# Two sibling edits joined: the end of the convolution module, the dilated closing, and a fifth place for weight units

## The chip, the cores and the metric

The kernel runs on one core of one Trainium2 chip. The metric is the device time of one execution in microseconds; several executions are taken and their median is compared. A profile of one execution stands beside them.

## The reference

Two transformer blocks of two layers each run over 512 tokens of 1024 features, all in float32. What matters here, shortened:

```python
for l in range(2):                                    # first block
    x = x + rmsnorm(mixer(rmsnorm(x)) @ w_out, norm_mix_post[l])
    x = x + rmsnorm(conv_gated_mlp(rmsnorm(x)), norm_ffn_post[l])
# second block, layer 0: conformer module
u = h @ w_in + b_in
u = u[..., :1024] * sigmoid(u[..., 1024:])
u = causal_dwconv(u, dw, dw_b)                        # 31 taps for each channel
u = silu(layer_norm(u, ln_g, ln_b))
x = x + rms_norm(u @ w_out + b_out, mix_post_g)
x = x + rms_norm(conv_ffn(rms_norm(x)), ffn_post_g)
# layer 1: dilated attention of 8 heads, then @ w_o, then the same feed-forward
```

## The kernel before, in words

Every product is done in three matmuls of a high and a low part (fp32r): x high by w high, x high by w low (or the reverse), x low by w high. Weights come from one packed tensor `in_wall` in the order of `PLAN`, eight 128 x 128 tiles to a unit. `dma_to` (L265 on) loads a unit on SyncE's queue into one of three `raw` tiles; `split_to` makes its two parts, a copy on ScalarE (L301) and a subtraction on VectorE (L302), ahead of the unit's use. Ordinary units go into four `w` tiles. Units marked keep go into tiles that `keeper` gives, since they are used while the four `w` tiles hold other units: the last four units of each closing, and the first four after it. `hold` says up to which unit kept ones may be split yet; `behind` names, for ScalarE and VectorE, an instruction behind which the steps of kept units are queued (`queue_behind`).

The program is a sequence of stages: mixer, feed-forward (`ffn`), mixer, feed-forward, `conformer`, feed-forward, `dilated`, feed-forward. Each ends in `closing`: a product with 1024 outputs, done for the first 256 tokens (h = 0), then for the other 256 (h = 1), each followed by `norms`: residual sum, post-norm, and `pre_norm`, which squares x, takes the inverse square root in some twelve small VectorE steps (`inv_sqrt`), makes xn (L473 on VectorE, L477 on ScalarE), transposes it on PE (htp, L488) and splits it into hh (L728) and hl (L729). `head` then runs the first six output tiles of the next stage over both halves. The last feed-forward has no next stage; its last two token tiles end in `last_norm` (L443 on), which adds, squares, multiplies by the gain in place (L451), and writes out.

In `conformer` eight channel tiles pass `conv_inputs`. Tiles 0 to 2 are summed tap by tap on VectorE (`tap_sums`, L1325), tiles 3 to 7 by matmuls with banded matrices on PE (`conv`, L1349), whose input cup is a rearranged copy of cu made by 16 small transfers (L1301). Each finished tile vc is transposed (ctp), copied to vt by token (L1369, L1334) and enters the statistics (L1373, L1336). Then come the aggregates (L1378), the inverse square root, and the normalisation of vt, q = 0 and 2 on VectorE (L1393), q = 1 and 3 on ScalarE (L1389). `silu_tiles` transposes back (ltp, L1236), applies silu (L1241) and splits into ch and cl, and the closing's matmuls (L555 to L557) use them.

In `dilated` the heads run first, then `close_begin` does the first four of the closing's eight steps while the last head's softmax runs, and `closing` the rest.

What order the instructions take on an engine is fixed when the program is built, by a planner that works with estimated times and keeps dependencies; on the chip each engine takes its instructions in that order. The generators of norms and convolutions are called in turns by a clock of spent PE time (`spend`, `tick`), which sets the order in which the code offers its work to the planner.

Of the kernel before, what the change touches and what calls it, by code (L numbers as in the profile page):

```python
# [28 lines left out]
P = 128  # L29
# [13 lines left out]

CONV_M, CONV_PAD = 9, 8

CONV_DVE, CONV_TAP = 3, 1.0
AX_LANES, AX_SOFTMAX, AX_NEXT, AX_PROB = 2, 5.5, 2.0, 1.7
AX_PM = 4
WIN_LANES, WIN_NEXT, WIN_SOFTMAX, WIN_PROB = 2, 2.0, 3.9, 1.4
# [175 lines left out]
class Kernel:  # L225
# [217 lines left out]
    def last_norm(self, t, banks, y, gain):  # L443

        nc = self.nc
        sums = self.sm.tile([P, 2, 2], F32, tag="sums", name="sums", bufs=4)[:, :1]
        halves = [(y[:, t, n * S : (n + 1) * S], slice(n * S, (n + 1) * S)) for n in range(2)]
        for n, (to, _) in enumerate(halves):
            nc.vector.tensor_tensor(to, to, banks[n], op=OP.add)
            self.square(to, sums[:, 0, n : n + 1])  # L450
        nc.vector.tensor_tensor(y[:, t], y[:, t], gain, op=OP.mult)  # L451
        rs = self.rms(sums)
        for n, (to, cols) in enumerate(halves):
            nc.vector.scalar_tensor_tensor(
                self.x[:, t, cols], to, rs[:, 0:1], self.x[:, t, cols], op0=OP.mult, op1=OP.add
            )
            queue = nc.scalar if n else nc.sync
            queue.dma_start(self.out[t * P : (t + 1) * P, cols], self.x[:, t, cols])

    def pre_norm(self, h, gain, wait=(0.0, 0.0)):  # L460
# [9 lines left out]
        for i in range(2):  # L470
            xn.append(self.sp.tile([P, D], F32, tag="xn", name="xn", bufs=2))
            if i:
                last = nc.vector.tensor_scalar(  # L473
                    xn[i], self.x[:, 2 * h + i], rs[:, i : i + 1], None, op0=OP.mult
                )
            else:
                last = nc.scalar.activation(  # L477
                    xn[i], self.x[:, 2 * h + i], AF.Copy, scale=rs[:, i : i + 1]
                )
            if h == 0 and self.n_unit:  # L480
                self.behind[last.ins.engine] = last.ins
        yield NORM_SUM[h] + NORM_NEXT
        at = slice(h * HS, (h + 1) * HS)
# [126 lines left out]
            self.close_some(xs, units, banks, 0, [k], [(0, 0), (0, 1), (1, 0)], 0, KD - 1)  # L610
        return banks, units

    def closing(self, w, l, xs, y, gain, pre, bias=None, ready=None, begun=None):


        groups, last = out_groups(len(xs))
# [3 lines left out]
        with self.tc.tile_pool(name="tail", bufs=1, reuse_waits="tile") as tp:  # L620
# [6 lines left out]
            else:  # L627
                banks, units = begun
            done = len(units)
            self.hold = self.n_unit + KD - done  # L630
            for k in range(done, KD):
                units += self.take_units(gemm_tiles(w, l, range(8), [last[k]]))
                if ready is not None:
# [25 lines left out]
    def ffn(self, up, down, l, taps, shifts, cb, act, post, pre):  # L659
        nc, tc = self.nc, self.tc  # L660
        groups, last = out_groups(NFF)
        with (
            tc.tile_pool(name="ffn", bufs=1, reuse_waits="tile") as fp,
            tc.tile_pool(name="taps", bufs=1, reuse_waits="tile") as qp,
        ):
            y = fp.tile([P, 4, D], F32, tag="y", name="y")
            gain = self.row(fp, post)

# [42 lines left out]
            for i, ks in enumerate(groups):  # L711
                got = group(ks)
                self.close_group(down, l, ks, got, y, i == 0)
                acts += got
            acts += group(last)
            with tc.tile_pool(name="kept", bufs=1, side="right", reuse_waits="tile") as tp:
                self.keeper(tp, "wt", 4)
                self.closing(down, l, acts, y, gain, pre)


    def split_out(self, hi, lo, src, scale=None):
# [434 lines left out]
    def mixer(self, l):  # L1156
        nc, tc = self.nc, self.tc
        with tc.tile_pool(name="mix", bufs=1, reuse_waits="tile") as yp:
# [35 lines left out]
            with tc.tile_pool(name="merged", bufs=1, reuse_waits="tile") as gp:  # L1194
                mh = gp.tile([P, KD, S], F32R, tag="mh", name="mh")
                ml = gp.tile([P, KD, S], F32R, tag="ml", name="ml")
                gain = self.row(gp, f"norm_mix_post{l}")
                self.branch(l, 2, yc, macc, False, (mh, ml))
                self.keeper(yp, "ys", 4)
                y = yp.tile([P, 4, D], F32, tag="macc", name="y")  # L1200
                self.closing(
                    "w_out", l, [(mh[:, k], ml[:, k]) for k in range(KD)], y,
                    gain, f"norm_ffn_pre{l}",
                )


# [46 lines left out]
    def conv_inputs(self):  # L1253
# [54 lines left out]
        def tap_sums():  # L1308
            for j in range(CONV_DVE):
# [26 lines left out]
                    nc.vector.bn_stats(stats[:, q, j], by[:, q])  # L1336
                summed.append(j)

        def conv():
            for j in range(CONV_DVE, KD):  # L1340
                while min(j + 1, KD - 1) not in phased:
                    yield 0.5
                if j == KD - 1:
                    yield 2.0
                ps = self.psum("a", "conv")
                for i in range(4):
                    w = mats[j][:, i]
                    for m in range(CONV_M):
                        nc.tensor.matmul(  # L1349
                            ps[:, i * P : (i + 1) * P], w[:, m].rearrange("p a b -> p (a b)"),  # L1350
                            phased[j][:, i, CONV_PAD - m : CONV_PAD - m + P],
                            start=m == 0, stop=m == CONV_M - 1, skip_group_check=True,
                        )
                    self.spend(CONV_M * 0.218)
                    yield 0.0
                if j + 2 < KD:
                    matrices(j + 2)
                vc = cv.tile([P, 4, P], F32, tag="vc", name="vc", bufs=3)
                nc.vector.tensor_tensor(
                    vc, ps.rearrange("p (i s) -> p i s", i=4),  # L1360
                    bias[:, 4 * j : 4 * j + 4, None].to_broadcast([P, 4, P]), op=OP.add,
                )
                yield 1.5
                pt = self.psum("a", "ctp")
                for i in range(4):
                    nc.tensor.transpose(pt[:, i * P : (i + 1) * P], vc[:, i], self.ident)
                self.spend(0.45)
                by = pt.rearrange("s (i q c) -> s q i c", i=4, q=4)
                nc.scalar.activation(  # L1369
                    vt[:, :, j * P : (j + 1) * P].rearrange("s q (i c) -> s q i c", i=4), by, AF.Copy  # L1370
                )
                for q in range(4):
                    nc.vector.bn_stats(stats[:, q, j], by[:, q])  # L1373
            while len(summed) < CONV_DVE:
                yield 0.3
            mv = self.sm.tile([P, 4, 2], F32, tag="lmv", name="lmv")
            for q in range(4):
                nc.vector.bn_aggr(mv[:, q], stats[:, q].rearrange("p a b -> p (a b)"))  # L1378
# [5 lines left out]
            nc.vector.scalar_tensor_tensor(  # L1384
                sh, mv[:, :, 0], -1.0, rs, op0=OP.mult, op1=OP.mult
            )
            for q in range(4):
                if q % 2:
                    nc.scalar.activation(  # L1389
                        vt[:, q], vt[:, q], AF.Identity, scale=rs[:, q : q + 1], bias=sh[:, q : q + 1]  # L1390
                    )
                else:
                    nc.vector.tensor_scalar(  # L1393
                        vt[:, q], vt[:, q], mv[:, q, 0:1], rs[:, q : q + 1],
                        op0=OP.subtract, op1=OP.mult,
                    )

        matrices(CONV_DVE)
        matrices(CONV_DVE + 1)
# [149 lines left out]
    def dilated(self):  # L1549
        with self.tc.tile_pool(name="dily", bufs=1, reuse_waits="tile") as yp:  # L1550
# [1 line left out]
            yl = yp.tile([P, KD, S], F32R, tag="dyl", name="dyl")  # L1552
            xs = [(yh[:, k], yl[:, k]) for k in range(KD)]
            gain = self.row(yp, "mix_post_g1")
            begun = self.dilated_heads(xs)
            with self.tc.tile_pool(name="kept", bufs=1, side="right", reuse_waits="tile") as tp:
                self.keeper(tp, "wt", 4)
                y = tp.tile([P, 4, D], F32, tag="y", name="y")
                self.closing("w_o", 0, xs, y, gain, "ffn_pre_g1", begun=begun)

    def dilated_heads(self, xs):
        nc, tc = self.nc, self.tc
# [222 lines left out]
```

## Time and profile before

| | us |
| --- | --- |
| median of 3 executions | 3178.2 (3178.11 to 3181.9) |
| the profiled execution | 3177.36 |
| its span, first to last instruction | 3175.6 |
| PE busy | 3103.4 |
| VectorE busy | 1828.9 |
| ScalarE busy | 1360.2 |

Busy times are unions of an engine's instructions. Matmuls follow each other before the earlier ones end, so a busy PE is one that has work under way. Times in the rows are microseconds from the span's start; line numbers are those of the kernel before.

### The profile page before, as it was taken

To read this page: it belongs to the slowest core of one execution; us is meant where nothing else is said; L and a number is where in the kernel's file an instruction comes from. 1 tells how busy PE (TensorE), PEld (TensorE's weight loads), DVE (VectorE), ACT (ScalarE), POOL (GpSimd) and SP (SyncE) were. 2 spreads that over 40 slices of the span, in tenths; PEclk is the share of its full clock that TensorE was granted. 3 is DMA by queue.
4 is the path that set the end of the run, shared out by engine and by line. 5 is a ranking of instruction groups with operands and counts; after the bars stand their busy time and mean duration, and the time that the engine had idled before them with its cause. 6 is when DMAs were issued, how large, how long until landed. Compare 5 with 4: busy or idle time off the path is not lost. (4 is left out here: it accounts for less than half of the span.)

```text
span 3175.6 us, 40474 instructions
## 1 busy us (share of the span) xinstructions
PE 3103.4 (98%) x15764; PEld 2609.7 (82%) x15764; DVE 1828.9 (58%) x3337; ACT 1360.2 (43%) x2231; POOL 337.1 (11%) x350
## 2 busy tenths in 40 slices
PE   8999999999999999999999989999999999999998
PEld 7788888888878888888888878888888888888887
DVE  6778346455676754555556865456545545464555
ACT  5566244334456643444334244334533333353332
POOL 0211100000011111000000000000143333100000
PEclk9999999999999999999999999999999999999999
DMA  4222232333311223233324422333222222223332
GB/s 139 67 77 84 94 106 85 95 100 94 99 64 60 90 90 107 79 100 98 95 93 161 152 87 73 97 95 120 74 87 73 75 86 80 74 87 99 95 99 73
DMA packets 86543, 293.84 MB, mean 93 GB/s; under 512 B 11088, under 2 KB 13904, under 8 KB 86352
## 3 DMA queue, kind: packets, MB, share of 16 engines
q1 hardware_dynamic: 82896, 278.41, 27.4%
q10 hardware_dynamic: 3456, 12.85, 1.1%
q8 instruction: 124, 2.03, 0.3%
q14 instruction: 67, 0.55, 0.0%
HBM read 287.81 MB, written 2.10 MB: 91 GB/s over the span
## 5 line engine op out<-in xcount | busy, mean ns | idle before, releaser
L345 PE MATMUL mm<-hh,w 128*128 128x512 f32 (+1 forms) x2720 | 1051.3, 386 | 0.0
L347 PE MATMUL mm<-hh,w 128*128 128x512 f32 (+1 forms) x2720 | 1035.7, 381 | 0.0
L346 PE MATMUL mm<-hl,w 128*128 128x512 f32 (+1 forms) x2720 | 1035.0, 381 | 0.0
L302 DVE TENSOR_TENSOR w<-raw,w 128x1024 fp32r<-128x1024 f32 x436 | 570.4, 1309 | 431.0 <-ACT w L301 426.4
L347 PEld LDWEIGHTS mm<-hh,w 128*128 128x128 f32 x2720 | 511.6, 188 | 97.0 <-issue 1.9
L346 PEld LDWEIGHTS mm<-hl,w 128*128 128x128 f32 x2720 | 512.4, 188 | 89.7 <-issue 1.9
L345 PEld LDWEIGHTS mm<-hh,w 128*128 128x128 f32 x2720 | 512.1, 188 | 89.8 <-issue 1.9
L301 ACT ACTIVATE w<-raw 128x1024 fp32r<-128x1024 f32 x436 | 458.5, 1053 | 236.8 <-PE mm L557 172.1
L679 DVE SCALAR_TENSOR_TENSOR cg<-mm,vecs,cg 128x511 f32<-128x511 f32 (+1 forms) x176 | 131.9, 749 | 207.0 <-ACT cg L672 204.3
L557 PE MATMUL mm<-w,al 128*128 128x512 f32 x576 | 224.7, 390 | 0.0
L555 PE MATMUL mm<-w,ah 128*128 128x512 f32 x576 | 224.6, 390 | 0.0
L556 PE MATMUL mm<-w,ah 128*128 128x512 f32 x576 | 224.6, 390 | 0.0
L679 DVE SCALAR_TENSOR_TENSOR cv<-mm,vecs,cv 128x511 f32<-128x511 f32 (+1 forms) x176 | 131.9, 749 | 103.9 <-ACT cv L672 101.2
L282 POOL TENSOR_TENSOR raw<-raw,vecs 128x1024 f32<-128x1024 f32 x66 | 132.7, 2012 | 545.4 <-DMA raw<-in_wall 503.7
L672 ACT ACTIVATE cg<-mm,vecs 128x512 f32<-128x512 f32 x88 | 68.6, 780 | 276.8 <-PE mm L347 276.8
L424 POOL TENSOR_TENSOR y<-y,row 128x512 f32<-128x512 f32 x18 | 23.3, 1311 | 1385.8 <-ACT junk L403 1385.8
L346 PE MATMUL mm<-hl,keep 128*128 128x256 f32 x512 | 144.9, 285 | 0.7 <-DVE hl L729 0.4
L347 PE MATMUL mm<-hh,keep 128*128 128x256 f32 x512 | 144.6, 284 | 0.0
L345 PE MATMUL mm<-hh,keep 128*128 128x256 f32 x512 | 143.2, 285 | 0.0
L555 PEld LDWEIGHTS mm<-w,ah 128*128 128x128 f32 x576 | 108.1, 188 | 23.2 <-issue 0.8
L556 PEld LDWEIGHTS mm<-w,ah 128*128 128x128 f32 x576 | 108.1, 188 | 22.4
L557 PEld LDWEIGHTS mm<-w,al 128*128 128x128 f32 x576 | 108.2, 188 | 22.2
(292 smaller groups left out, 4374.3 us busy)
## 6 DMA issues: line engine op xcount, KB each, us to landing
raw<-in_wall SPq DMA_DIRECT2D x500, 512.0 KB, 3.5
cw<-in_cm_mats ACTq DMA_DIRECT2D x20, 576.0 KB, 6.5
row<-in_rows SPq DMA_DIRECT2D x9, 512.0 KB, 4.3
bias<-in_rpb SPq DMA_DIRECT2D x16, 256.0 KB, 3.6
x<-in_x SPq DMA_DIRECT2D x4, 512.0 KB, 5.9
cup<-cu SPq DMA_DIRECT2D x80, 16.0 KB, 1.8
out<-x SPq DMA_DIRECT2D x4, 256.0 KB, 2.1
out<-x ACTq DMA_DIRECT2D x4, 256.0 KB, 2.1
```

The costliest lines, as they stand in the source:

```text
L282: self.nc.gpsimd.tensor_tensor(rows, rows, g[:, k0 : k0 + ks, None].to_broadcast(list(rows.shape)), op=OP.mult)
L301: nc.scalar.activation(hi, raw, AF.Copy),
L302: nc.vector.tensor_tensor(lo, raw, hi.bitcast(F32), op=OP.subtract),
L345: nc.tensor.matmul(ps, wh, xh, start=first and i == 0, stop=False, **check)
L346: nc.tensor.matmul(ps, wh, xl, start=False, stop=False, **check)
L347: nc.tensor.matmul(ps, wl, xh, start=False, stop=stop, **check)
L424: nc.gpsimd.tensor_tensor(to, to, gain[:, cols], op=OP.mult)
L555: nc.tensor.matmul(ps, xh, wh, start=first, stop=False)
L556: nc.tensor.matmul(ps, xh, wl, start=False, stop=False)
L557: nc.tensor.matmul(ps, xl, wh, start=False, stop=last)
L672: nc.scalar.activation(o, ps, AF.Identity, scale=self.vec(taps + str(k0), f), bias=self.vec(cb, f))
L679: nc.vector.scalar_tensor_tensor(o[:, to], ps[:, of], self.vec(taps + str(k), f), o[:, to], op0=OP.mult, op1=OP.add,)
```

## The change

Six edits, in the order of the diff. `last_norm` multiplies each half by its part of the gain as soon as the half is summed, into a tile of its own. At the program's start the VectorE instruction that makes xn enters `behind`, so the subtractions of the first kept units come after it. `closing` takes a number `spare`: kept units may be split that many units further; with five kept tiles in the feed-forwards (the tiles of the taps are freed before, to make room) and a fifth tile in the mixers, the first unit after the closing is split before the closing's norms. In the conformer the transposes of a convolved tile come between the quarters of the next convolution; the taps' interval in the generators' clock is 0.9 instead of 1.0; behind the last tile come one silu of a column and 36 transposes on PE into a bank that nothing reads; the normalisation is done in column halves, and its last steps enter `behind`. In `dilated` one kept tile lies beside the heads' tiles, and the closing's first kept unit may be split before the heads end.

```diff
-CONV_DVE, CONV_TAP = 3, 1.0
+CONV_DVE, CONV_TAP, WARM = 3, 0.9, 36
...
+        scaled = []
         for n, (to, _) in enumerate(halves):
             nc.vector.tensor_tensor(to, to, banks[n], op=OP.add)
             self.square(to, sums[:, 0, n : n + 1])
-        nc.vector.tensor_tensor(y[:, t], y[:, t], gain, op=OP.mult)
+            scaled.append(self.sp.tile([P, S], F32, tag="xn", name="scaled", bufs=4))
+            nc.vector.tensor_tensor(scaled[n], to, gain[:, n * S : (n + 1) * S], op=OP.mult)
...
-            if h == 0 and self.n_unit:
+            if h == 0 and (self.n_unit or i):
                 self.behind[last.ins.engine] = last.ins
...
-            self.hold = self.n_unit + KD - done
+            self.hold = self.n_unit + KD - done + spare
...
+            taps_pool.close()
             with tc.tile_pool(name="kept", bufs=1, side="right", reuse_waits="tile") as tp:
-                self.keeper(tp, "wt", 4)
-                self.closing(down, l, acts, y, gain, pre)
+                self.keeper(tp, "wt", 5)
+                self.closing(down, l, acts, y, gain, pre, spare=1)
...
+                four, own, count = self.keep, gp.tile([P, 4, S], F32R, tag="wt", name="keep"), [0]
+                def place():
+                    count[0] += 1
+                    return own.rearrange("p a b -> p (a b)") if count[0] == 5 else four()
+                self.keep = place
...
+        waiting = []
+        def by_token(j, vc):
+            pt = self.psum("a", "ctp")
+            for i in range(4):
+                nc.tensor.transpose(pt[:, i * P : (i + 1) * P], vc[:, i], self.ident)
...
                     self.spend(CONV_M * 0.218)
+                    if i == 1 and waiting:
+                        by_token(*waiting.pop())
                     yield 0.0
...
+                waiting.append((j, vc))
+            yield 1.5
+            by_token(*waiting.pop())
             while len(summed) < CONV_DVE:
                 yield 0.3
+            early = cv.tile([P, 1], F32, tag="early", name="early")
+            nc.scalar.activation(early, vc[:, 0, :1], AF.Silu)
+            spare = self.psum("b", "warm")
+            for _ in range(WARM):
+                nc.tensor.transpose(spare[:, :P], vc[:, 0], self.ident)
...
+            for n in range(2):
+                for q in range(4):
+                    part = vt[:, q, n * S : (n + 1) * S]
+                    if q % 2 and n == 0:
+                        last = nc.scalar.activation(
+                            part, part, AF.Identity, scale=rs[:, q : q + 1], bias=sh[:, q : q + 1]
+                        )
+                    else:
+                        last = nc.vector.tensor_scalar(
+                            part, part, mv[:, q, 0:1], rs[:, q : q + 1],
+                            op0=OP.subtract, op1=OP.mult,
+                        )
+                    self.behind[last.ins.engine] = last.ins
...
-            begun = self.dilated_heads(xs)
...
+            with self.tc.tile_pool(name="kept1", bufs=1, side="right", reuse_waits="tile") as op:
+                count = [0]
+                def place():
+                    first = count[0] % 4 == 0
+                    count[0] += 1
+                    pool, tag, bufs = (op, "wt1", 1) if first else (self.tp, "wt", 3)
+                    w = pool.tile([P, 4, S], F32R, tag=tag, name="keep", bufs=bufs)
+                    return w.rearrange("p a b -> p (a b)")
+                self.keep, self.hold = place, HEADS[6] - 3
+                begun = self.dilated_heads(xs)
```

## Rows read from the trace of the kernel before

**Rows 1.** The page, busy us of each engine, share of span, instructions.
```profile
PE 3103.4 (98%) x15764; PEld 2609.7 (82%) x15764; DVE 1828.9 (58%) x3337; ACT 1360.2 (43%) x2231; POOL 337.1 (11%) x350
```
**Rows 2.** PE's waits, whole span: waiter, releaser, us in total, times, longest.
```profile
PE htp L488 <- ACT xn L477: 26.6, 15, 13.9
PE ltp L1236 <- DVE vt L1393: 8.8, 1, 8.8
PE htp L488 <- DVE hl L729: 7.5, 7, 1.5
...
PE ctp L1366 <- DVE vc L1359: 2.7, 2, 1.9
```
**Rows 3.** Stretches: length, each engine's busy us (instructions), granted clock, DMA share, GB/s.
```profile
1819.00:1831.00 12.00, 1.91 (x12) 1.25 (x12) 11.69 (x35) 5.16 (x7) 0.00 (x0) 0.80 0.20 53
1831.00:1840.00 9.00, 6.58 (x24) 5.10 (x25) 3.77 (x6) 8.97 (x10) 0.00 (x0) 0.50 0.46 164
```
**Rows 4.** Timeline, conformer's end: start, us, engine, line, operation, count, [idle before, releaser].
```profile
1819.00 0.69 DVE L1359 TENSOR_TENSOR vc<-conv,cbias 128x512 f32<-128x512 f32 x1 [6.52 <-PE conv L1349]
1819.61 2.05 DVE L1325 SCALAR_TENSOR_TENSOR vc<-cw,vecs,cacc 128x512 f32<-128x512 f32 x2
...
1826.27 1.22 DVE L302 TENSOR_TENSOR keep<-raw,keep 128x1024 fp32r<-128x1024 f32 x1
...
1830.21 0.16 DVE L1384 SCALAR_TENSOR_TENSOR lsh<-lmv,lrs 128x4 f32<-128x4 f32 x1
...
1830.47 2.38 ACT L1389 ACTIVATE vt<-vt,lsh,lrs 128x1024 f32<-128x1024 f32 x2 [4.57 <-DVE lsh L1384]
...
1831.25 2.98 PE L1236 MATMUL ltp<-ident,vt 128*128 128x128 f32 x12 [8.81 <-DVE vt L1393]
...
1832.75 1.04 ACT L301 ACTIVATE keep<-raw 128x1024 fp32r<-128x1024 f32 x1
...
1833.81 1.28 ACT L1241 ACT_TABLE_LOAD   x1
...
1838.22 0.78 PE L555 MATMUL mm<-w,ch 128*128 128x512 f32 x1
```
**Rows 5.** The tile cup, 1795 to 1822 us: count, shortest/median/longest ns, first and last start.
```profile
L1349 PE MATMUL conv<-cup,cw x144: 270/275/275, 1800.2 to 1818.7; 128*128 128x128 f32 x144
L1301 SPq DMA_DIRECT2D cup<-cu x16: 512/589/1580, 1803.5 to 1813.9; - x16
...
DMA to landing us min/median/max: 1.8/1.8/3.5
```
**Rows 6.** Timeline, dilated closing.
```profile
2762.85 3.50 DVE L302 TENSOR_TENSOR keep<-raw,keep 128x1024 fp32r<-128x1024 f32 x3 [0.25 <-ACT keep L301]
...
2762.87 1.67 PE L555 MATMUL mm<-keep,dyh 128*128 128x512 f32 x6 [2.48 <-ACT keep L301]
```
**Rows 7.** Timelines of ScalarE, PE and VectorE, closing of the first feed-forward.
```profile
820.86 0.63 ACT L403 ACTIVATE junk<-y 128x512 f32<-128x512 f32 x1 [12.78 <-DVE y L415]
...
850.47 0.30 PE L488 MATMUL htp<-ident,xn 128*128 128x128 f32 x1 [1.13 <-DVE hl L729]
...
850.83 1.76 DVE L302 TENSOR_TENSOR w<-raw,w 128x1024 fp32r<-128x1024 f32 x1
...
866.44 0.33 PE L488 MATMUL htp<-ident,xn 128*128 128x128 f32 x1 [0.84 <-ACT xn L477]
```
**Rows 8.** Timeline, the program's start.
```profile
9.37 1.23 DVE L302 TENSOR_TENSOR keep<-raw,keep 128x1024 fp32r<-128x1024 f32 x1 [0.77 <-ACT keep L301]
9.55 1.06 ACT L301 ACTIVATE keep<-raw 128x1024 fp32r<-128x1024 f32 x1 [0.21 <-DMA raw<-in_wall]
...
10.98 1.23 DVE L302 TENSOR_TENSOR keep<-raw,keep 128x1024 fp32r<-128x1024 f32 x1
...
12.70 1.15 ACT L477 ACTIVATE xn<-x,rst 128x1024 f32<-128x1024 f32 x1 [0.33 <-DVE rst L373]
```
**Rows 9.** Timeline, the tail behind the last matmul.
```profile
3167.60 1.23 DVE L451 TENSOR_TENSOR y<-y,row 128x1024 f32<-128x1024 f32 x1 [0.85 <-ACT junk L403]
```

## What I predict, and why

> **What bounds the kernel now.** I read the page first: TensorE (PE) is busy 98% of the span [rows 1], so only its idle time is on offer: 3175.6 - 3103.4 = 72 us. The view of PE's waits shows where it lies [rows 2]: 26.6 us before the transposes of the pre-norms (htp, waiting for xn), 13.9 us of it at the very start; 8.8 us before the layer-norm transposes of the conformer (ltp, waiting for vt); 7.5 us in seven waits for hl; 2.7 us for the convolution's vc. 2.48 us for one kept weight unit stand in the dilated closing [rows 6], and the tail's chain comes behind the last matmul [rows 9]. The view of stretches shows one place where PE is also slow [rows 3]: 1831 to 1840 us ran at a granted clock of 0.50, the lower level, and 0.80 over the 12 us before says that it fell some 4.8 us ahead of 1831. Everywhere else an edit on another engine pays only if it shortens one of these waits. The timelines then show what ended each.
>
> **The change part by part.**
>
> *Conformer, end of the chain.* The last convolution ended at about 1818.97 (vc follows at 1819.00) and the first matmul of the closing started at 1838.22: 19.25 us [rows 4]. Three things leave this chain. (a) Three subtractions of kept units, 1.22 us each, sit between the small steps of the inverse square root. From 1826.27, where the first of them starts, to the last step (lsh) at 1830.21 it is 3.94 us; the five small steps in there, 0.16 us long and one each 0.2, need 1.0: 2.9 us. The new entries in `behind` put them after the normalisation. (b) ScalarE normalises two whole rows in 2.38 us; now two halves, 1.2 us, with VectorE's halves beside them: 1.2 us. The other halves go to VectorE (0.4 us each), and only the fifth silu tile on needs them. (c) The table load of 1.28 us before the first silu moves to the early silu, while ScalarE has only evacuations to do. Sum 5.4 us. The kept unit's copy at 1832.75, 1.04 us, also stood between; it must now come after ScalarE's last half, but in front of the silu is still free time, so I leave it there. Bounds: 4.1 us if the table load costs the statistics as much as it frees, 6.4 us if the copy moves too. The tap interval of 0.9 reorders the tap sums; their two last steps, 2.05 us, stand behind vc now while VectorE had been idle 6.5 us [rows 4]. I see no reason in the code that they pass vc, since places for vc are given in order; if they do it is 2.05 us more.
>
> *Conformer, the convolution itself.* The transposes of tile 6 now come between the quarters of convolution 7, so PE's wait of 1.9 us for vc [rows 2] goes. What is next late is the tile's own transfer [rows 5]: 16 issues on SyncE's queue from 1803.5 to 1813.9, landing 1.8 us after each. The last quarter can start at 1815.7 and takes 2.05 us (two convolutions in 18.8 us, less the wait and four transposes, by eight quarters), so it ends at 1817.75: 1.2 us gained, between 0 and 1.9.
>
> *Conformer, the 36 warming transposes.* They are new work on PE: at full clock 0.114 us each (the spacing of the convolution's records), 4.1 us; at half clock 0.25 us each (12 ltp in 2.98 us), 8.9 us. PE's idle stretch of 8.81 us begins 3.5 us after the convolution, and after (a), with half a row in front instead of a whole one, the first ltp can start 12.3 - 2.9 - 0.4 = 9.0 us after it [rows 4]. At full clock they end at 7.6 and are hidden; at half clock they end at 12.4, 3.4 us late. I count nothing. If they hold the clock, the four matmuls from 1838.22 on run 0.2 us each faster: 0.8 us more. The rows leave this open: 20 transposes between 1831 and 1838 ran at half clock and did not raise it, while it fell only after PE had stood still for some 3.8 us, not right after the last real matmul [rows 3, 4]. The Trainium skill (TensorE: Matmul & The Clock Gate, Part 4: PE-mode transpose) says that transposes don't count as busy for the clock, which speaks against this part of the change; the transposes at half clock agree with it, the late fall does not. By the rule the warming buys nothing and may itself run slow; by the other reading it gives 0.8 us.
>
> Conformer in all: 5.4 + 1.2 = 6.6 us, bounds 1 and 11.
>
> *Dilated closing.* One kept unit now has a place of its own during the heads and is split before they end. In the profile PE stood 2.48 us at 2762.87 for the first of three kept units, whose subtractions then took 3.50 us from 2762.85 on [rows 6]. With the first one ready, PE goes on at 2760.4 with its twelve matmuls of 0.23 us, until 2763.2; by then the next unit's copy is done and its subtraction ends about 2764.1, as now, with four matmuls that need only the copy ahead of it: 2764.1. So 2.4 us, bounds 1.2 and 2.5. The early split itself, 1.05 us on ScalarE and 1.22 on VectorE, falls among the last head's softmax, where PE has matmuls of the closing to do; without that cover it costs 1.2 us, the lower bound.
>
> *Fifth place in mixers and feed-forwards.* Five closings get it. The first head unit is then split ahead of the norms, into ScalarE's idle 12.78 us before 820.86, and its load slot serves the queue sooner (on SyncE: raw loads move up by one unit; nothing else waits on that queue there). Behind the norms one copy and one subtraction fewer compete with hh and hl. What this can take away is the wait for hl, as 1.13 us at 850.47 [rows 7]; seven such waits make 7.5 us [rows 2], four of them in these closings, one each in the mixers and the first two feed-forwards: 4 x 1.1 = 4.3 us. But the weight stream moves up as a whole: the subtraction at 850.83, 1.76 us with its wait for a load, may be replaced by the next one. And the transposes of the second half wait for xn anyway (0.84 us at 866.44): PE gains only what that chain gains. I take half, 2.1 us; bounds 6 (the later wait shrinks too) and -2.
>
> *Start.* The subtractions of the first kept units now come behind xn. Two of them, 1.23 us each at 9.37 and 10.98, hold up the small steps by some 2.5 us, so xn could start at 10.2 instead of 12.70 [rows 8]. ScalarE's second copy, 9.55 to 10.61, isn't moved and stands ahead: 2.1 us. Then hh shares ScalarE with squares of the second half: I take 1.8, bounds 0 and 2.5.
>
> *Tail.* The gain's product of 1.23 us over both halves waits for the square because it writes in place [rows 9]. Now the first half is done earlier and the second, into another tile, beside the square. At most the product's 1.23 us leave the chain; I take 1.1, bounds 0.9 and 1.2. The extra tiles are only memory.
>
> Sum: 6.6 + 2.4 + 2.1 + 1.8 + 1.1 = 14.0 us. The profiled execution took 3177.4 us (span 3175.6 and 1.8 around it), so 3163.4; the median of the runs, 3178.2, is 0.8 above it: **3164 us**.
>
> **The rivals.**
> *More comes.* The last taps pass vc, the warming holds the clock, the copy leaves the silu's way, xn's waits shrink: 2.05 + 0.8 + 1.04 + 3.9 = 7.8 us more, 3156 us. For it: VectorE's 6.5 us of idle time and a ScalarE with nothing else to do. Against: four things must agree.
> *The clock falls under the warming transposes.* They are the only work of PE after 1818, and the rows at half clock show that transposes don't raise it. They then end up to 3.4 us late, so 3167.5 us. It decides only if the clock falls while they still run; in the profile it fell 7.2 us after the convolution's end, when at full clock they would just be through. By the skill's rule named above it could.
> *The change doesn't do what it says.* The order of each engine's instructions is planned from estimated times, and new entries can leave other waits in the same places: the conformer keeps its chain but for the table load (1.3), hl and xn wait as now, the dilated unit and the tail give 2.4 + 1.1: 4.8 us, 3173.4 us, within 0.2%. For it: the wait for xn at 866.44, of 0.84 us, stands where PE still had matmuls of the first half left, so it is such an error.
> *Slower.* With one unit ahead, the stream of weight units reaches the second half's norms earlier, and two more splits per closing (1.06 on ScalarE, 1.22 on VectorE each) get in front of its sums, in the chain that PE waits for at 866.44. Price 2 x 2.28 = 4.6 us in five closings, 23 us, less the other 11.9: 3189 us. It decides from 2.4 us per closing on. Against it: the four slots for split units free only as PE finishes the closing, and there are as many as now.
>
> **How the numbers follow.** Forecast 0.58, between 3160 and 3168; more 0.14; clock under the warming 0.12; not what it says 0.11; slower 0.05. About 0.2%, 6.4 us, is what a measurement of this kernel can tell from no change: faster is below 3171.8. The first three are faster, 0.84; same 0.11; slower 0.05. The range for 8 in 10 leaves out the slow rival, most of the third and the far end of the first: 3156 to 3172.
>
> **What would show it.** Right: PE's wait at ltp falls from 8.8 us to some 5 with the transposes before it, no VectorE subtraction between statistics and lsh, the table load before the statistics end, no wait for keep at the dilated closing, xn at 10.6 at the start, no product between the last square and the last sum. The clock's fall, if any, shows in the row of 1819 on. Wrong: kept copies still in front of the first silu for several us, waits for the transfer of cu in convolution 7 over 0.7 us, or waits for xn that grow by what the waits for hl lose.

## The result, and the profile after

The changed kernel took **3161.84 us** (median of 4, 3161.18 to 3162.36), the kernel before 3179.74 us beside it: 17.9 us less, ratio 0.9943, 95% interval 0.9926 to 0.996. The forecast was 3164, 14 us less. The profiled execution of after took 3162.36 us, its span is 3160.6, 15.0 us less than before.

Here "before" and "after" name the kernel before and the changed kernel. The page of after, as [rows 1]; then PE's waits, as [rows 2] (waiter, releaser, us in total, times, longest):

```profile
PE 3107.4 (98%) x15800; PEld 2614.7 (83%) x15800; DVE 1833.0 (58%) x3343; ACT 1360.5 (43%) x2232; POOL 334.8 (11%) x350
```
```profile
PE htp L490 <- ACT xn L479: 22.9, 15, 11.9
PE htp L490 <- DVE hl L733: 5.5, 4, 2.6
...
PE ltp L1247 <- DVE vt L1421: 1.9, 1, 1.9
PE ltp L1247 <- ACT ct L1252: 1.3, 1, 1.3
...
PE ctp L1355 <- DVE vc L1386: 0.8, 1, 0.8
```

PE has 36 instructions and 4.0 us more to do and still ends 15 us earlier: its idle time fell from 72 to 53 us. The wait for a kept unit at the dilated closing is gone, that for vt fell from 8.8 to 1.9 us (with the warming in front of it), that for vc from 2.7 to 0.8. The waits for hl are fewer, but one of them, 2.6 us, is longer than any in the kernel before.

The conformer's end, as [rows 4] (start, us, engine, line, operation, count, [idle before, releaser]):

```profile
1807.28 4.18 PE L1374 MATMUL conv<-cup,cw 128*128 128x128 f32 x36
...
1808.09 1.28 ACT L1398 ACT_TABLE_LOAD   x1
...
1811.50 0.69 DVE L1386 TENSOR_TENSOR vc<-conv,cbias 128x512 f32<-128x512 f32 x1 [2.50 <-PE conv L1374]
1812.11 2.05 DVE L1336 SCALAR_TENSOR_TENSOR vc<-cw,vecs,cacc 128x512 f32<-128x512 f32 x2
...
1814.76 3.77 PE L1401 MATMUL warm<-ident,vc 128*128 128x128 f32 x33
...
1819.65 0.16 DVE L1410 SCALAR_TENSOR_TENSOR lsh<-lmv,lrs 128x4 f32<-128x4 f32 x1
...
1819.91 1.52 ACT L1417 ACTIVATE vt<-vt,lsh,lrs 128x512 f32<-128x512 f32 x2 [4.35 <-DVE lsh L1410]
...
1820.42 1.87 PE L1247 MATMUL ltp<-ident,vt 128*128 128x128 f32 x12 [1.89 <-DVE vt L1421]
1821.34 1.04 ACT L301 ACTIVATE keep<-raw 128x1024 fp32r<-128x1024 f32 x1
...
1825.38 0.78 PE L557 MATMUL mm<-w,ch 128*128 128x512 f32 x1
```

From the convolution's end at 1811.46 to the first matmul of the closing it is 13.92 us now, 19.25 before: no subtraction stands between the statistics and lsh, the table load has moved ahead of the last vc, the kept unit's copy still stands before the first silu. Convolutions 6 and 7 run through without a wait, since cup comes early enough now (as [rows 5], last issue at 1806.8 and the last quarter of the convolution only after it):

```profile
L1374 PE MATMUL conv<-cup,cw x144: 270/275/275, 1794.3 to 1811.2; 128*128 128x128 f32 x144
L1312 SPq DMA_DIRECT2D cup<-cu x16: 512/589/1135, 1796.9 to 1806.8; - x16
...
DMA to landing us min/median/max: 1.8/1.8/3.9
```

The clock, as [rows 3] (length, each engine's busy us, granted clock, DMA share, GB/s):

```profile
1812.00:1820.40 8.40, 5.84 (x48) 5.20 (x49) 7.99 (x33) 2.48 (x5) 0.00 (x0) 1.00 0.01 2
1820.40:1825.38 4.98, 3.65 (x20) 2.83 (x21) 4.04 (x8) 4.98 (x7) 0.00 (x0) 0.62 0.13 35
1825.38:1830.00 4.62, 4.62 (x16) 3.70 (x15) 3.83 (x6) 4.62 (x6) 0.00 (x0) 0.67 0.37 116
1877.00:1884.00 7.00, 4.40 (x27) 4.22 (x27) 5.69 (x8) 5.04 (x11) 2.19 (x2) 0.76 0.43 139
```

It stayed at full speed under all warming transposes, fell during the ltp transposes, was back at 1828.5, and fell again in the closing, at about 1879.7. There stands the place where most time was lost: PE's wait of 2.60 us for hl, behind a split on ScalarE that waited for its load:

```profile
1878.21 1.06 ACT L301 ACTIVATE w<-raw 128x1024 fp32r<-128x1024 f32 x1 [1.76 <-DMA raw<-in_wall]
1879.17 0.46 ACT L732 ACTIVATE hh<-htp,vecs 128x256 fp32r<-128x256 f32 x1
...
1880.30 0.66 PE L490 MATMUL htp<-ident,xn 128*128 128x128 f32 x2 [2.60 <-DVE hl L733]
```

The other places, as [rows 6 to 9]: the dilated closing's first kept matmuls run on without a wait while the three subtractions of the later units follow; in the first feed-forward's closing ScalarE's idle 12.78 us became 10.01 and PE's wait for hl 0.75 instead of 1.13; at the start xn begins at 10.68 and PE at 11.86 instead of 13.90; in the tail the gain's product stands beside the square.

```profile
2752.07 3.50 DVE L302 TENSOR_TENSOR keep<-raw,keep 128x1024 fp32r<-128x1024 f32 x3 [0.26 <-ACT keep L301]
2752.94 1.34 PE L557 MATMUL mm<-keep,dyh 128*128 128x512 f32 x5
...
817.79 0.63 ACT L403 ACTIVATE junk<-y 128x512 f32<-128x512 f32 x1 [10.01 <-DVE y L415]
846.88 0.52 PE L490 MATMUL htp<-ident,xn 128*128 128x128 f32 x3 [0.75 <-DVE hl L733]
...
10.68 1.14 ACT L479 ACTIVATE xn<-x,rst 128x1024 f32<-128x1024 f32 x1
11.86 1.76 PE L490 MATMUL htp<-ident,xn 128*128 128x128 f32 x7 [11.86 <-ACT xn L479]
...
3152.79 0.69 DVE L453 TENSOR_TENSOR scaled<-y,row 128x512 f32<-128x512 f32 x1
```

Matmul by matmul (the same matmul's start in both traces), after is ahead of before by 1.4 us after the start, 3.0 after the first mixer's closing, 4.1, 5.4 and 5.2 after the next three, 12.8 at the conformer closing's first matmul, 12.2 a few matmuls later, where the clock was down, 9.8 to 10.8 behind that closing, 13.4 in the dilated closing, 14.0 behind it and 15.0 at the end. The open questions were the 2 us lost between the first matmul of the conformer's closing and its end, and what the warming does.

### The profile page after: what moved, and what is told of

Read it like the earlier page. It is cut to its first block, busy times and chain, and to the rows that moved or that the text cites. A ratio compares the mean times of both kernels' runs of the same rounds, so it can differ in the third digit from the quotient of the medians.

```text
span 3160.6 us, 40570 instructions
## 1 busy us (share of the span) xinstructions
PE 3107.4 (98%) x15800; PEld 2614.7 (83%) x15800; DVE 1833.0 (58%) x3343; ACT 1360.5 (43%) x2232; POOL 334.8 (11%) x350
## 4 chain that ended last, share of the span: by engine, by line
PE 83%; DVE 9%; ACT 4%; issue 2%; DMA 1%; POOL 0%; SPq 0%; DVEq 0%; ACTq 0%; POOLq 0%
PE mm L347 18%; PE mm L345 18%; PE mm L346 18%; PE mm L557 5%; PE mm L559 5%; PE mm L558 5%; ACT junk L403 2%; DVE w L302 2%; DMA raw<-in_wall 1%; PE z L345 1%; PE z L347 1%; PE z L346 1%; PE conv L1374 1%; PE pt L930 1%; PE dpo L1515 1%
```

## The experiments

**One part at a time.** Four kernels, each the kernel before with one group of the edits. They share 27 runs of before, median 3178.76 us.

```diff
 e1: WARM, taps' interval 0.9, by_token, early, warm, halves, behind in conformer
 e2: spare, wt 5, place() in mixer          (fifth place)
 e3: kept1, place() in dilated
 e4: scaled in last_norm; (self.n_unit or i) in pre_norm
```

> The kernel before with the conformer's edits alone (convolved tile transposed between the quarters, tap interval 0.9, early silu, 36 warming transposes, column halves, entries in behind). My terms: 6.6 us less than before. Reading of the two traces: the first matmul of the conformer's closing comes 7.3 us earlier, the closing itself then loses some 2 us in a wait for hl (2.60 us, behind a ScalarE split that waits for a raw load). Theory A, the loss belongs to the edit (the closing starts earlier than its loads): 5.3 us less in time, and a wait of PE for hl of over 2 us in the conformer's closing. Theory B, the late load was an accident of one execution: 7.3 us less, the wait for hl about 1.4 us as before.

> The kernel before with the fifth place for kept units alone (mixers and feed-forwards, spare 1). My term: 2.1 us less (bounds -2 and 6). The two traces read closing by closing: 1.6, 1.05, 1.3, then twice about 0: 3.6 us less. Theory A (the waits for hl go, and later waits don't take their place): 3.6 us less, PE's waits for hl fall from 7.5 us to some 4. Theory B (half is given back): 2 us less. Rival (the weight stream two splits ahead): slower.

> The kernel before with the dilated edit alone (one kept place during the heads). My term: 2.4 us less, bounds 1.2 and 2.5; the wait for keep of 2.48 us at the dilated closing gone. Rival: the early split, 1.05 us on ScalarE and 1.22 us on VectorE, delays the last head's softmax: 1.2 us less.

> The kernel before with the start (VectorE's xn enters behind) and the tail (the gain's product by halves into tiles of its own) alone. My terms: 1.8 + 1.1 = 2.9 us less. The two traces: 1.4 + 1.0 = 2.4 us less; PE's first htp at 11.9 us instead of 13.9, of which 0.6 us is given back later in the first stage. Rival (the start's gain is lost wholly in the first stage): 1.0 us less.

| edits | median us | runs | less than before | 95% interval of the ratio |
| --- | --- | --- | --- | --- |
| conformer | 3168.42 | 6 | 10.3 | 0.9956 to 0.9981 |
| fifth place | 3174.79 | 10 | 4.0 | 0.9979 to 0.9998 |
| dilated | 3175.96 | 10 | 2.8 | 0.9981 to 0.9999 |
| start and tail | 3176.09 | 10 | 2.7 | 0.9984 to 1.0002 |

Together 19.8 us, where all in one gave 17.9, and 15.6 when it was measured again (below). The intervals are 6 to 8 us wide, so the sizes have to be read from the traces. The stages that a kernel leaves alone show how far traces differ by themselves: ahead of the conformer, at 1684 us, the three kernels without the fifth place were 1.0 to 1.8 us ahead of the profiled execution of before, and the one with it 4.0. So the fifth place gave 2.3 to 3.0 us there, between the two theories of e2, and its waits for hl are four, 4.3 us, where the others have six to eight, 5.9 to 6.8 us. All 14 traces of this document say the same: from 40 to 1684 us the ten with the fifth place gain 3.8 us on the mean on the profile of before, the three others 1.5, so 2.3 us are the edit's. The conformer alone (e1) was 9.4 us ahead at its closing's first matmul, 1.4 of it from the stages ahead of the conformer, and gained 0.8 more over the next few, for its clock didn't fall there. In its closing it lost nothing: its wait for hl there was 1.03 us. Theory B held in this wait, and the interval of its time, 6 to 14 us less, holds B's 7.3 and not A's 5.3. With all edits the 2 us needed another reason.

Stretches of e1 behind the warming; then the dilated closing in e1, which still has the wait for a kept unit, and in e3, which has not (the granted clock stands ahead of the last two numbers):

```profile
1822.05:1824.22 2.17, 0.28 (x3) 0.07 (x2) 1.90 (x10) 0.51 (x1) 0.00 (x0) 1.00 0.00 0
1824.22:1828.85 4.63, 2.70 (x21) 2.07 (x21) 3.69 (x7) 4.63 (x7) 0.00 (x0) 1.00 0.10 16
```
```profile
2750.00:2758.00 8.00, 6.37 (x21) 5.06 (x22) 4.75 (x5) 4.53 (x5) 0.00 (x0) 0.79 0.50 142
```
```profile
2750.00:2763.00 13.00, 12.42 (x73) 10.44 (x72) 7.12 (x25) 3.97 (x9) 2.37 (x4) 1.00 0.00 0
```

In e3 the lead over before grows by 2.75 us where the wait stood: the term of 2.4 held, the rival of 1.2 did not. The wait of 2.5 us in the dilated closing let the clock fall in the traces of e1, e2 and e4, and not in that of before; these three lose 1.5 to 2.6 us of their lead there. The edit that removes the wait also removes that.

Of the start and the tail together, 2.7 us was measured, 2.9 had been counted, and the interval goes down to no gain. The trace of e4 shows less. PE began at 11.96 instead of 13.90, but then waited 1.30 us for hl at 32.28, where before it waited 0.38 us at 31.37, and at 40 us only 0.05 us of the lead was left: the rival. Behind the last matmul the tail was 1.1 us shorter (8.4 instead of 9.55 us). The ten traces that have the start's edit lie between 0.3 us behind before and 1.6 us ahead of it at 40 us, with a median of 0.3. The 1.4 us of the first profile of after is near the top of these.

**The same kernel again, and three changes at the conformer's end.**

> The changed kernel once more, unaltered. In its first profile the conformer's closing lost some 2 us: a wait for hl of 2.60 us, behind a ScalarE split that waited 1.76 us for a raw load, and a second fall of the clock. With the conformer's edits alone that wait was 1.03 us. Theory A (accident of one execution): wait for hl about 1 us, no second fall, span some 2 us below 3160.6 unless it falls elsewhere. Theory B (all edits together bring the closing ahead of its loads): again over 2 us.

```diff
-                    self.behind[last.ins.engine] = last.ins      (e6)
```

> The changed kernel without the conformer's entry in behind, so that three subtractions of kept units stand between the steps of the inverse square root again. My term (a): 2.9 us slower than the changed kernel. If the clock then falls under the longer wait as it did before, up to 1 us more: 3.9. Rival: the subtractions were only moved behind the normalisation, into silu's way, and cost as much there: 0 to 1 us.

```diff
-CONV_DVE, CONV_TAP, WARM = 3, 0.9, 36
+CONV_DVE, CONV_TAP, WARM = 3, 0.9, 32
-                nc.tensor.transpose(spare[:, :P], vc[:, 0], self.ident)
+                nc.tensor.matmul(spare[:, :P], vc[:, 0], self.ident, start=True, stop=True)
```

> The changed kernel with 32 float32 matmuls (0.228 us each by the convolution's records, 7.3 us together) in place of the 36 warming transposes (4.1 us); they end about 1.9 us before the first ltp is ready plus or minus 2. Theory A (transposes hold the clock as matmuls do; what lets it fall is PE standing still): no difference beyond 1 us, the fall moves with the end of the warming work. Theory B (transposes don't hold it, it fell late by chance): the granted clock stays at 1.0 through the conformer's end in this kernel, 1 to 2 us faster than the changed kernel.

```diff
-CONV_DVE, CONV_TAP, WARM = 3, 0.9, 36
+CONV_DVE, CONV_TAP, WARM = 3, 0.9, 0
```

> The changed kernel without the 36 warming transposes. My count: 0 (if they hold the clock, 0.8 us). Theory A (they hold it): the clock falls before the ltp transposes, which then take 0.25 us instead of 0.11 each, eight of them in the chain (1.1 us), and the first matmuls of the closing run at half clock (0.8 us and more): 1.9 to 3 us slower than the changed kernel. Theory B (they don't count): within 0.5 us of it, and the same stretch at half clock.

Four runs each, median: again 3162.66 (3159.12 to 3164.18), kept in chain 3164.16, real matmuls 3161.21, **no warming 3159.29** (3158.97 to 3161.45); before beside them 3178.26. From the start of the last convolution's last record (0.3 us ahead of its end) to the first matmul of the closing:

| | chain us | clock there | wait for hl in the closing | last piece of the raw load behind it |
| --- | --- | --- | --- | --- |
| after | 14.2 | fell during ltp | 2.60 | 6.2 us |
| after again | 13.87 | did not fall | 2.51 | 6.1 |
| real matmuls | 13.92 | did not fall | 2.35 | 6.0 |
| kept in chain | 16.93 | fell during ltp, back before the closing | 0.79 | 4.4 |
| no warming | 13.86 | fell 3.7 us before ltp | 1.15 | 4.3 |

The lines of e6, of VectorE and of PE's wait:

```profile
1819.00 1.22 DVE L302 TENSOR_TENSOR keep<-raw,keep 128x1024 fp32r<-128x1024 f32 x1
...
PE ltp L1247 <- DVE vt L1421: 4.9, 1, 4.9
```

Three readings. (1) The entry in `behind` is worth 2.7 to 3.1 us of the chain (16.93 against 14.2 and 13.87 in the two profiles of after), 2.9 counted: in e6 three subtractions of 1.22 us stand between the steps again and PE waits 4.9 us for vt. Its time is only 1.5 to 2.3 us longer, since its closing has the short wait.

(2) The warming keeps the clock up and shortens nothing. Without it the clock fell before ltp, but the chain was as long, and the clock was back before the first matmul of the closing:

```profile
1817.30:1821.00 3.70, 0.00 (x0) 0.03 (x1) 3.29 (x18) 0.51 (x1) 0.00 (x0) 0.50 0.00 0
1821.00:1824.10 3.10, 3.03 (x12) 2.22 (x12) 3.10 (x6) 3.10 (x5) 0.00 (x0) 0.50 0.00 0
1824.20:1828.00 3.80, 3.44 (x17) 2.56 (x18) 2.14 (x5) 3.80 (x5) 0.00 (x0) 1.00 0.45 138
```

Both theories of e8 missed: A said 1.9 to 3 us slower, B the same time, and it was 2 to 3 us faster. Of its lead over the first profile of after, 1.2 us came over the first matmuls of the closing, where the clock of after was down, 1.4 us in the closing, and 0.9 us in stages behind it that both have alike. At the lower level the ltp transposes take 2.61 us for 12 instead of 1.34, but PE had waited for silu behind them (1.56 us in the second execution of after, 0.16 without warming), so ScalarE covers it. The real matmuls of e7 don't tell its two theories apart: the clock stayed up under them, but with the transposes it did so too in the second execution of after.

(3) The late load was no accident of one execution (theory B of e5): it came in both executions of after and with real matmuls, and not in e1 and e6, which also have the 36 transposes, nor without them. What it was, the records of the trace tell: a raw load lands in 16 pieces. Of the load issued at 1871.97 in after, 15 had landed after 4.4 us and the last after 6.2. Meanwhile PE's own instructions were fetched: one packet of 16 KB, at 1875.2, 3.2 us behind the issue. The rows show the load, the fetch in the stretch from 1874 to 1877, and the same queue over the whole run (packets, MB, share of 16 engines):

```profile
L269 SPq DMA_DIRECT2D raw<-in_wall x1: 328/328/328, 1872.0 to 1872.0; - x1
...
DMA to landing us min/median/max: 6.2/6.2/6.2
```
```profile
q8 instruction: 1, 0.02, 1.9%
...
q8 instruction: 124, 2.03, 0.3%
```

Over all 14 profiles of this case, 39 of 7000 raw loads have a last piece more than 1.2 us behind the other 15. In 39 of the 39, and in 16% of all, such a fetch began between 1 us before the issue and the landing. That is 1087 loads with a fetch beside them, of which 1048 had no late piece. The Trainium skill (Runtime: NRT & Kernel Launch, Instruction fetch mechanics) says that an engine's instructions are refilled in 16 KiB blocks of 256, and that the cost of one is mostly hidden. The blocks agree: PE has 31,942 records in after, its sequencer's included, some 257 for each of the 124 packets. At the fetch of 1875.2 PE too shows no stop (busy all the time from 1874.5 to 1876.5). Where PE's instructions come in such blocks, 36 transposes with their weight loads, 72 instructions, should shift each later fetch against the work; without warming the fetch came at 1879.1, 8 us behind the issue at 1871.08 and long after that load had landed. That the fetch is what holds up the piece is not shown by this: the two are only seen together.

**Is it the place of the fetch?** In e9 the 36 transposes were put where PE stands still anyway, at the start, and none behind the convolution; e10 has half of them.

```diff
-CONV_DVE, CONV_TAP, WARM = 3, 0.9, 36
+CONV_DVE, CONV_TAP, WARM = 3, 0.9, 0
...
+            spare = self.psum("b", "warm")
+            for _ in range(36):
+                nc.tensor.transpose(spare[:, :P], self.ident, self.ident)
             with tc.tile_pool(name="start", bufs=1, side="right") as sp:
```

> The changed kernel with its 36 transposes not behind the last convolution but at the very start, on the identity tile, where PE stands still for 11.9 us; nothing else moves. Every PE instruction from there to the conformer thus has as many before it as in the changed kernel from the warming on. In the trace of the changed kernel the raw transfer issued at 1871.97 landed 15 of its 16 pieces after 4.4 us and the last after 6.2 us, while a fetch of 16 KB of PE's instructions ran at 1875.2; without the warming the fetch came at 1879.1 and the piece was not late. Theory A (where the instruction fetch falls costs the 2 us): the wait for hl in the conformer's closing is again over 2 us, and the time is that of the changed kernel, 3162 us, give or take what the start costs. Theory B (the warming itself costs it, or chance): wait for hl about 1.1 us, 3159.3 us as without warming.

```diff
-CONV_DVE, CONV_TAP, WARM = 3, 0.9, 36
+CONV_DVE, CONV_TAP, WARM = 3, 0.9, 18
```

> The changed kernel with 18 warming transposes instead of 36. Theory A (place of the instruction fetch): it moves by some 36 PE instructions against the raw transfers, so the late piece goes or meets the next transfer, which has time: wait for hl about 1.1 us, about 3159.5 us. Theory B (the warming as such costs time): half the loss, 3160.7 us. In both the first matmul of the closing comes 13.8 us after the last convolution's end, as with 36 and with none.

e9 brought the late piece back without any warming in the conformer: the fetch at 1873.4, the load issued at 1869.89, its last piece at 5.8 us (15 of them by 4.3), the wait for hl 2.14 us. Its rows, the raw transfer and PE's wait, and the raw transfer and PE's wait of e8 below:

```profile
L269 SPq DMA_DIRECT2D raw<-in_wall x1: 327/327/327, 1869.9 to 1869.9; - x1
DMA to landing us min/median/max: 5.8/5.8/5.8
...
1877.75 0.41 PE L490 MATMUL htp<-ident,xn 128*128 128x128 f32 x2 [2.14 <-DVE hl L733]
```
```profile
L269 SPq DMA_DIRECT2D raw<-in_wall x1: 327/327/327, 1871.1 to 1871.1; - x1
DMA to landing us min/median/max: 4.3/4.3/4.3
...
1877.96 0.41 PE L490 MATMUL htp<-ident,xn 128*128 128x128 f32 x2 [1.15 <-DVE hl L733]
```

The long wait of theory A came and its time did not: 3159.59 us (3159.22 to 3160.65), not 3162. Against after, e9 was 0.7 us ahead before the conformer and 1.3 us more over the first matmuls of the conformer's closing, where in the profiled execution of after the clock was down; its closing then lost less (0.9 us of its lead, where after lost 1.4; 2.14 us of wait, not 2.60). The four traces with the late load lose 0.9 to 1.4 us in this closing, the others nothing: that is its price, less than the 2 us of theory A, and executions differ by more. e10, with half the warming, had its wait for hl back at 0.80 us and took 3160.57 us (3159.14 to 3162.6), between the two theories; its fetch came 3.5 us behind the issue of the load and yet no piece was late. In the four late cases it came 3.0 to 3.5 us behind, in e1 and e6 2.8; there no piece was late by this measure, though in e6 the last one was 1.1 us behind. So no late piece stands here without a fetch beside its load, but a fetch doesn't by itself make one. What more it takes stays open.

**The two other terms, and a further step.** Both without warming; the rows show what each changes beyond that.

```diff
-            nc.scalar.activation(early, vc[:, 0, :1], AF.Silu)    (e11)
-            for n in range(2):
+            for n in range(1):                                    (whole rows, part = vt[:, q])
```

> The changed kernel without warming, without the early silu, and with the normalisation in whole rows as before. My terms (b) and (c): 1.2 + 1.28 = 2.5 us longer from the last convolution's end to the first matmul of the closing, 16.25 us instead of 13.75. Rival: the first ltp needs all four rows' first columns anyway and VectorE had the time, so halves give less than 0.5 us: 15.2 us.

```diff
+                if j == 0:
+                    self.behind[copied.ins.engine] = copied.ins   (copied: the copy to ch, e12)
```

> The changed kernel without warming, and with the copies of kept units queued behind the first copy ch of the silu tiles on ScalarE: the kept unit's copy of 1.04 us, which stands between the normalisation and the first silu, goes behind. The chain from the last convolution's end to the first matmul of the closing: 13.75 - 1.04 = 12.7 us, and about 3158.3 us in time. Rival: silu then waits for the ltp transposes, 0.1 to 0.6 us at the lower clock, and half the gain goes: 13.2 us.

e11: the chain is 16.48 us instead of 13.86, 2.62 longer, where 2.5 was counted; the table load of 1.28 us stands before the first silu again, and two whole rows take 2.37 us on ScalarE, two halves 1.52 (so (b) is 0.85 there, not 1.2; the other 0.5 us stands behind them, where the clock, down until 1834, is still low at the first matmul). Its one run took 3165.93. The two lines of ScalarE:

```profile
1821.98 2.37 ACT L1416 ACTIVATE vt<-vt,lsh,lrs 128x1024 f32<-128x1024 f32 x2 [4.36 <-DVE lsh L1409]
...
1825.32 1.28 ACT L1252 ACT_TABLE_LOAD   x1
```

e12 gained 0.25 us of the chain (13.61), not 1.04, and not the half that the rival left: with the copy gone, silu waits 0.57 us for the ltp transposes, which run at the lower level, and the copy to ch still stands behind the second silu, as it does without this edit. ScalarE in e12:

```profile
1820.59 1.52 ACT L1416 ACTIVATE vt<-vt,lsh,lrs 128x512 f32<-128x512 f32 x2 [4.36 <-DVE lsh L1409]
1822.67 2.31 ACT L1252 ACTIVATE ct<-ltp,vecs 128x512 f32<-128x512 f32 x2 [0.57 <-PE ltp L1247]
1824.77 0.65 ACT L1259 ACTIVATE ch<-ct 128x512 fp32r<-128x512 f32 x1
```

Its time, 3160.11 us (3159.95 to 3162.14), isn't better than that without warming alone. The two together, the copy behind and warming that doesn't put the fetch beside the load, weren't tried. The lowest median here is that of the change without its warming: 3159.29 us, 2 to 3 us below the changed kernel, with ranges that touch; those of e9 and e12 lie within 1 us of it.

## Why the prediction was right

The sign and the size held: 14.0 us counted, 15.0 read from the two traces, 3164 forecast and 3161.84 measured. By medians it was 17.9 us, and 15.6 the second time. The signs came too: without the warming PE's wait at ltp is 5.5 us (e8), "some 5" had been said, and PE's waits for xn did not grow (11.0 us behind the start in after, 12.7 in before). By its steps:

- **Conformer's chain**, 5.4 counted, 5.3 measured (19.25 to 13.92). From the timelines of before and after, (a) is 3.05 where 2.9 was counted, (b) 0.86 where 1.2 was (two half rows take ScalarE 1.52 us, not 1.2), and (c) with the steps up to the first matmul 1.42 where 1.28 was. So the sum is closer than its terms. The experiments agree: 2.7 to 3.1 for (a) in e6, 2.62 for (b) and (c) in e11, with a lower clock in it. The copy stayed in front of silu and the two tap steps behind vc (1812.11), as said; that the copy costs its 1.04 us there fell in e12: the ltp transposes are late next.
- **Convolution**, 1.2 counted, 1.9 measured by PE's wait for vc (2.7 to 0.8), the upper bound, and 2.3 by the traces (5.2 ahead at the first convolution on PE, 7.5 at the last one's end). The step that failed is "what is next late is the tile's own transfer", taken with its times of [rows 5]: the issues came 7.1 us earlier (last one 1806.8 instead of 1813.9) while the work ahead of them had moved by some 5.5, so the last quarter found its data.
- **Warming**, counted at nothing. As hidden work that was right: the transposes ran at full clock and ended 2 us before ltp. The rival in which the clock falls under them did not come about. But the choice between 0 and a gain of 0.8 left out that 36 instructions may also change things elsewhere: in both profiles of after the wait for hl in the conformer's closing was 2.5 to 2.6 us instead of about 1.1, and the closing gave back 1.3 to 1.4 us of what the conformer had gained. In the first of them 0.6 us more went with the clock at the closing's first matmuls. That the warming is the cause is not shown: e1 and e6 have it without the long wait, and e9 has the long wait without it.
- **Dilated**, 2.4 counted, 2.7 measured by the traces (10.8 to 13.5 ahead) and 2.8 by medians, a little over its upper bound of 2.5; the prediction did not see that the wait may also take the clock with it.
- **Fifth place**, 2.1 counted, 2.3 to 3.0 by the traces at 1684 us, 2.3 by the mean of all traces, 4.0 by medians with an interval of 0.6 to 6.7: "I take half" was about right. The rival of a stream two splits ahead did not show: behind the start, PE's waits for xn are 10.5 us in all in e2 and 12.7 in before.
- **Start** 1.8 counted. PE came 2.04 us earlier, and a new wait of 0.5 us for a kept subtraction (PE mm for keep, at 18.80) took part of it back; 1.4 us were left in the first profile of after. But in e4 nothing was left at 40 us, and 0.3 is the median of ten traces: the term took the earlier start for a gain, and the later waits for hl, near 32 us, took most of it back. **Tail** 1.1 counted, 1.0 to 1.1 read.

The misses of single terms went both ways: the convolution's was 0.7 to 1.1 us too small, the start's over 1 us too large in most traces, and the conformer's closing gave back 2 us that were not counted. The 15.0 us also hold some 1.5 us by which the profile of before was slower, up to 1684 us, than those of other kernels in stages that these leave alone. That the sum came within 1 us is therefore partly luck; the mechanisms of the large terms are not.

## What to carry to other kernels

Read a chain's terms from the rows and move what doesn't belong in it; the chain's sum held to 0.1 us here, its terms to 0.4. Ask of a gain at the start of a stage whether the next wait in it takes it back: 2 us at PE's first instruction left 0.3. Before an engine's idle time is filled with work "for free", look at what comes later: here 36 instructions were hidden on PE, and a wait 1.4 us longer came with them in both profiles of the changed kernel, beside a fetch of PE's instructions and a weight load with no time to spare; whether the fetch is the cause is not settled. And where gains of 1 to 3 us are asked of a kernel whose executions spread over 1 to 7, compare stages in several traces and use an unchanged stage as the measure of chance.

## What the hardware showed unexpectedly

- A fetch of 16 KB of PE's instructions stands beside every one of the 39 late pieces of 512 KB loads, which came up to 2.3 us behind the other 15; of the 1087 loads with such a fetch beside them, 1048 had none.
- The clock came back under transposes alone. Without warming it was at the lower level from 1817.3 and back at 1824.1, with 12 ltp transposes since 1821.0 as PE's only work, and the first real matmul at 1825.64; in e10 likewise, from 1821.3 to 1824.7 with the first matmul at 1825.78, and in e6, e9 and e12 too. In [rows 3, 4] 20 transposes, with a pause of 2.2 us among them, had not brought it back. The Trainium skill (TensorE: Matmul & The Clock Gate, Part 4: PE-mode transpose) says that a transpose doesn't count as PE-busy the same way; these rows speak against it as a rule for these float32 transposes, as does the full clock through 36 of them.
- Whether the clock falls at one and the same place differs from execution to execution: in the conformer it fell in one profile of after and not in the other, and at the dilated closing's wait of 2.5 us in three traces (e1, e2, e4) and not in that of before.
